# Holding the first expert's low-part subtracts back behind the first row gather, clearing two row tiles in mid-routing, and loading one pair of down weights later

## The chip, the cores and the metric

The kernel runs on one core of one Trainium2 chip. The metric is device time in microseconds (us) of one execution; 0.5% of it is 5.96 us. One execution was also taken by the hardware profiler, and its rows give start and length of each instruction on TensorE (PE, and PEld for its weight loads), VectorE (DVE), ScalarE (ACT), GpSimd (POOL) and SyncE (SP), and the landing of the transfers.

## The reference

A decoder block on x of 1024 rows by 1024 columns: a parallel pair of mixers (forgetting attention and a diagonal state space model), then a mixture of experts. Only the second half of it meets the change:

```python
def _hier_moe(x, w_rg, b_rg, w_re, b_re, w_gate, w_up, w_down):
    g_prob = jax.nn.softmax((xt @ w_rg) + b_rg)          # 4 groups
    g_top, g_sel = lax.top_k(g_prob, 1)
    e_prob = jax.nn.softmax(e_in)                        # 8 experts of that group
    e_top, e_idx = lax.top_k(e_prob, TOP_K)              # two of them
    w = g_top * e_top / jnp.sum(e_top, axis=-1, keepdims=True)
...
    for e in range(N_EXPERTS):                           # 32
        h = jax.nn.silu(xt @ w_gate[e]) * (xt @ w_up[e])
        y = y + combine[:, e:e + 1] * (h @ w_down[e])
# in the block:  x = x + mixed @ w_out;  x = x + _hier_moe(_rmsnorm(x, norm_ffn_g), ...)
```

An expert's gate and up weights are 1024x256 each, its down weights 256x1024.

## The kernel before

**Routing.** The output product `mixed @ w_out` runs over 8 row tiles of 128 rows, two halves of 512 columns each: 16 units, numbered `u`, one call of `product` each. Behind a tile's two units its `tail` runs: the finished rows go to `out_rows`, the norm's factor `rstd` is formed, the router's logits go through a long chain of small VectorE operations (group, two experts, position of the row within each expert), and the normed rows `xn` are stored to `xn_d` in DRAM. After the last tile the list `ix` is complete: for each of the 32 experts the numbers of up to 96 rows that chose it (line 1313).

**Experts.** They are taken in the order `ORDER`; "expert 0" below is the first in that order. For each: an indirect DMA on GpSimd's queue (`gather_rows`, L1330) fetches its rows of `xn_d` into a row tile `XG` that was cleared before (MEMSET, L1323); `turn_rows` transposes them on TensorE (L1341) and ScalarE and VectorE split the result into a high part `xh` (L1344) and a low part `xl` (L1345); `gate_up` multiplies them with the weights in three products: high x high (L1354), high x low weights (L1355), low x high (L1356), 24 matmuls in 8 steps; `hidden` forms `si` and `hh`; `down` multiplies with the down weights `wd` (L1379), and GpSimd adds the rows to `out_rows` (L1381, an indirect DMA too). Three row tiles rotate.

**Weights.** `load_expert` issues six loads of 512 KB on SP's queue for each expert: four `raw_e` (gate and up, L1085) and two `wd` (L1089). Five sets of buffers rotate. `split_expert` turns the four `raw_e` into high parts `weh` (8 casts on ScalarE, L1103) and low parts `wel` (8 subtracts on VectorE, L1104: raw less high). Once both have read a `raw_e` tile, the load of the expert five places later may overwrite it.

**Order.** The loads of the first experts start during routing, at the units that `AHEAD` lists ({unit: [(expert, loads)]}). `issue_after` (here through `after`) holds an instruction in its engine's stream until a named one has been issued; within an engine the order is then fixed. At routing's end, before: the two XG memsets, gather 0, gather 1, the third memset; on VectorE `ix`, `wts`, and then all of expert 0's subtracts.

Of the kernel before, what the change touches and what calls it, by code (L numbers as in the profile page):

```python
# [10 lines left out]
F32 = mybir.dt.float32  # L11
F32R = mybir.dt.float32r
# [4 lines left out]
ALU = mybir.AluOpType  # L17
AX = mybir.AxisListType

P = 128  # L20
D = 1024
S = 1024
# [20 lines left out]
def hybrid_block(ctx: ExitStack, tc: tile.TileContext, t, out):  # L43

    nc = tc.nc

    def pool(stack, name, bufs=1, side=None, space=None):
        kw = {}
        if side:
            kw["side"] = side  # L50
        if space is not None:
            kw["space"] = space
        return stack.enter_context(tc.tile_pool(name=name, bufs=bufs, **kw))
# [6 lines left out]
    def mmtile():  # L60
        return psA.tile([P, 512], F32, tag="A", name="psA_t")
# [4 lines left out]
    def f32(ap):  # L66
        return ap.bitcast(F32)
# [4 lines left out]
    def slot(name, shape=(S,), dt=F32, where=None):  # L72
        pl, n = where or (slab, SLOTS)
        return pl.tile([P] + list(shape), dt, tag="s4", name=name, bufs=n)
# [12 lines left out]
    sp = pool(ssm_stack, "ssm_c", 1, side="right")  # L87
# [265 lines left out]
    for nm, dst in (("ssm_C_re", Cre), ("ssm_C_im", Cim)):  # L353
        cin = tp.tile([P, 4, 2, 64], F32, name="cin", bufs=2)
        src = t[nm].rearrange("(b a) c p -> (a c) b p", a=8)
# [132 lines left out]
    with ExitStack() as st:  # L488
# [19 lines left out]
        for b in range(G // GB):  # L508
# [4 lines left out]
            v = wp2.tile([P, GB, P], F32, name="v", tag="t1")  # L513
# [79 lines left out]
            for q4 in range(GB // 4):  # L593
# [7 lines left out]
                for r in range(4):  # L601
                    g = q4 * 4 + r
                    o = ps[:, r * P:(r + 1) * P]
# [13 lines left out]
    with ExitStack() as st:  # L617
# [23 lines left out]
        for m in range(4):  # L641
            ms = slice(m * P, m * P + P)
            for n in range(2):
                ns = slice(n * 512, n * 512 + 512)
                ps = smtile()
                for k in range(4):
                    wh, wl = [w_[:, k % 2, ms] for w_ in wgl_[k // 2]]
# [332 lines left out]
    SR = (slabR, SLOTSR)  # L980
# [92 lines left out]
    def load_expert(e, raws, wd):  # L1073
# [13 lines left out]
        for j in range(2):  # L1087
            wd[j] = wd[j]()
            tc.keep_in_program_order(nc.sync.dma_start(wd[j], wd3[:, j, :]))  # L1089
            yield raws, wd  # L1090

    def split_expert(raws, c):

        ws = []
        for k2 in range(4):
            v = (2 * c + k2 // 2) % 3, k2 % 2
            if v not in ws_t:
                ws_t[v] = slot("weh", (2, 512), F32R), slot("wel", (2, 512), F32R)
            wh, wl = ws_t[v]
            for q in range(2):  # L1100
                src = raws[k2 // 2 * 2 + q][:, k2 % 2 * 2:k2 % 2 * 2 + 2, :]
                d_ = (slice(None), slice(None), slice(q * 256, q * 256 + 256))
                nc.scalar.copy(wh[d_], src)  # L1103
                nc.vector.tensor_tensor(wl[d_], src, f32(wh[d_]), ALU.subtract)  # L1104
            ws.append((wh, wl))
            if k2 == 1:
                yield
        yield ws
# [3 lines left out]
    def place_of(nm, shape, tiles, c, where):  # L1112
        def get():
            if c not in tiles:
# [7 lines left out]
    raw_t, wd_t, ws_t = {}, {}, {}  # L1122
    ahead = [load_expert(ORDER[o], [place_of("raw_e", (4, 256), raw_t, (SET[o], q), RAW[SET[o]][q]) for q in range(4)],
                         [place_of("wd", (S,), wd_t, (o % 5, j), WD[o % 5][j]) for j in range(2)]) for o in range(NE)]
    got = []
    AHEAD = {0: [(0, 6)], 2: [(1, 6)], 8: [(2, 6)], 12: [(3, 6), (4, 2)], 14: [(4, 2)]}

    ix = rp.tile([CAP, NE], I32, name="ix")
    wts = rp.tile([CAP, NE], F32, name="wts")
    empty = rp.tile([P, NE], F32, name="empty")  # L1130
    cnt = rp.tile([P, NE], F32, name="cnt")
    ptab = mmtile()
    with ExitStack() as st:
        xp = pool(st, "x1p", 1, side="right")
# [16 lines left out]
        def product(i, n):  # L1151
            if i not in x1s:
                x1s[i] = slot("x1", where=(SR, S2)[i - NT + 2]) if i >= NT - 2 else xp.tile([P, D], F32, name="x1", bufs=2)
                nc.gpsimd.dma_start(x1s[i], t["x"][i * P:(i + 1) * P, :])
            x1 = x1s[i]
            ns = slice(n * 512, n * 512 + 512)
            ps = mmtile()
            for k in range(KD):
                if k == KD // 2:
                    yield  # L1160
                mh, ml = [v[k // 4, i // 2][:, k % 4, i % 2 * P:i % 2 * P + P] for v in (mxh, mxl)]
                wh, wl = [v[:, k % 2, :] for v in wos[n, k // 2]]
                nc.tensor.matmul(ps, mh, wh, start=(k == 0), stop=False)  # L1163
                nc.tensor.matmul(ps, mh, wl, start=False, stop=False)
                nc.tensor.matmul(ps, ml, wh, start=False, stop=(k == KD - 1))
            nc.vector.tensor_tensor(x1[:, ns], ps, x1[:, ns], ALU.add)
# [113 lines left out]
        ends = {}  # L1280
# [3 lines left out]
        def behind_products(u):  # L1284

            if 0 < u <= len(units):
                i = units[u - 1][0]
                next(tails.setdefault(i, tail(i)))
            if u > 1 and units[u - 2] in done:
                next(tails[units[u - 2][0]], None)  # L1290

        done = [u for o, u in enumerate(units) if u[0] in [v[0] for v in units[:o]]]
        for u, (i, n) in enumerate(units):
            for o, m in AHEAD.get(u, ()):
                for _ in range(m):
                    r_ = next(ahead[o])
                got[o:] = [r_]
            pr = product(i, n)
            next(pr)
            if u == 1:  # L1300
                out_splits(3)
            behind_products(u)
            for _ in pr:
                pass
        behind_products(len(units))
        behind_products(len(units) + 1)
        for _ in range(2):
            r_ = next(ahead[4])

# [3 lines left out]
        last_dve = nc.vector.tensor_tensor(ix, ptab[0:CAP, 0:NE], empty[0:CAP], ALU.add)  # L1313
# [2 lines left out]


    em_ = pool(ctx, "moe", 1, side="right")
    XG = []

    def rows_tile(where):
        XG.append(where.tile([P, S], F32, name="XG") if where is em_ else slot("XG", where=where))
        nc.gpsimd.memset(XG[-1], 0.0)  # L1323

    rows_tile(SR)
    rows_tile(SR)
    mt = pool(ctx, "moet", 2, side="right")

    def gather_rows(xg, ix):
        return nc.gpsimd.indirect_dma_start(out=xg[0:CAP], out_offset=None, in_=xn_d[:, :],  # L1330
                                     in_offset=bass.IndirectOffsetOnAxis(ap=ix, axis=0),
                                     bounds_check=S - 1, oob_is_err=False)

    def turn_rows(xg):

        xh = mt.tile([P, KD, CAP], F32R, name="xh")
        xl = mt.tile([P, KD, CAP], F32R, name="xl")
        for kk in range(2):
            ps = smtile()
            for r in range(4):  # L1340
                pe = nc.tensor.transpose(ps[:, r * CAP:(r + 1) * CAP], xg[0:CAP, kk * 4 + r::8], ident[0:CAP, 0:CAP])  # L1341
            dst = (slice(None), slice(kk * 4, kk * 4 + 4))
            pv = ps[:, 0:4 * CAP].rearrange("p (a b) -> p a b", a=4)
            nc.scalar.copy(xh[dst], pv)  # L1344
            nc.vector.tensor_tensor(xl[dst], pv, f32(xh[dst]), ALU.subtract)  # L1345
        return (xh, xl), pe

    def gate_up(x, ws):
        xh, xl = x
# [40 lines left out]
    def icol(o):  # L1390
        return ix[:, ORDER[o]:ORDER[o] + 1]


    def after(*instructions):

        st = ExitStack()
        for ins in instructions:
            st.enter_context(tc.issue_after(ins.ins))
        return st

    for o in range(2):
        last_gather = gather_rows(XG[o], icol(o))
    with tc.issue_after(last_gather.ins):
        rows_tile(em_)
    w_now = got[0]
    got.append(r_)
    got.extend([None] * (NE - 5))

    def load(o, n):
        if o < NE:  # L1410
            for _ in range(n):
                got[o] = next(ahead[o])
    with after(ends["act"], last_dve):
        *_, ws = split_expert(got[0][0], 0)
    load(5, 4)
    x, _ = turn_rows(XG[0])
    sp = split_expert(got[1][0], 1)
    next(sp)
    load(6, 2)
    behind, act, dve = None, ends["act"], last_dve  # L1420
    scs = []
    for o in range(NE):
        if o + 2 < NE:
            gather_rows(XG[(o + 2) % 3], icol(o + 2))
        ps, pe = gate_up(x, ws)
        if o + 1 < NE:
            w_next = got[o + 1]
            if o:
                with after(act, dve):
                    sp = split_expert(w_next[0], o + 1)  # L1430
                    next(sp)
                load(o + 6, 2)
        h = hidden(ps)
        dve = next(h)
        if o + 1 < NE:
            with after(pe):
                x, pe = turn_rows(XG[(o + 1) % 3])
        if behind:
            with after(pe):
                _, sc, pe = down(*behind, apart=scs[-3:])  # L1440
            scs.append(sc)
            load(o + 4, 2)
        with after(pe):
            hT, act = next(h)
        e = ORDER[o]
        behind = (hT, w_now[1], icol(o), wts[:, e:e + 1])
        if o + 1 < NE:
            with after(act, dve):
                ws = next(sp)
            load(o + 6, 2)  # L1450
        w_now = w_next
# [13 lines left out]
    with tc.If(nb > 1):  # L1465
# [10 lines left out]
        with tc.For_i(1, nb, 1) as b:  # L1476
            with tc.For_i(0, NE, 1) as e:
                ne = nc.values_load(cnti[0:1, bass.ds(e, 1)], min_val=0, max_val=S)
                with tc.If(ne > b * CAP):
# [7 lines left out]
                    raws, wd = list(load_expert(e, [place_of("raw_e", (4, 256), raw_t, (0, q), None) for q in range(4)],  # L1487
                                                [place_of("wd", (S,), wd_t, (0, j), None) for j in range(2)]))[-1]
# [29 lines left out]
```

## Time and profile before

| what | value |
|---|---|
| median of 3 runs | 1191.19 us (1191.03 to 1195.45) |
| the profiled execution's own time | 1195.19 us |
| its span, first to last instruction | 1193.5 us (1.69 us lie around it) |
| PE busy | 1111.4 us, 93% of the span |
| DVE, ACT, POOL busy | 67%, 52%, 36% |
| bytes moved | 193.78 MB, mean 162 GB/s |

The profiled execution is 4.0 us (0.34%) longer than the median of the runs. The share of a busy engine is an average over very different stages: the routing ends at about 839 us, and the experts follow until the end.

### The profile page before, as it was taken

How to read it: one execution, taken by the hardware profiler on the slowest of the kernel's cores; microseconds unless marked ns; L12 is line 12 of the kernel's file. 1: busy time of each engine (PE TensorE's matmuls, PEld its weight loads, DVE VectorE, ACT ScalarE, POOL GpSimd, SP SyncE). 2: the span in 40 equal slices, each digit the busy share in tenths (PEclk: the TensorE clock that was granted, in tenths of full speed). 3: DMA queues.
4: the chain of work that ended last, by engine and by line, in shares of the span. 5: the costliest groups of instructions: out<-in, count | busy, mean ns of one | idle time of the engine just before them, and what ended most of it. 6: DMA issues, size and time to landing. Idle time of an engine off the chain costs nothing. (4 is left out here: it accounts for less than half of the span.)

```text
span 1193.5 us, 15934 instructions
## 1 busy us (share of the span) xinstructions
PE 1111.4 (93%) x5323; PEld 851.5 (71%) x5324; DVE 795.3 (67%) x1561; ACT 620.3 (52%) x1195; POOL 431.3 (36%) x431
## 2 busy tenths in 40 slices
PE   5999989899999999999899989998599999999995
PEld 4778877787898878888667767886366666666562
DVE  4976786575027889898986795538566666666661
ACT  5443232233226566756769453103466666666672
POOL 3143553541523564756624362103322222222211
PEclk9999999899999999999999998999699999999998
DMA  7625652330443020001523548564699999999992
GB/s 236 85 55 159 137 81 62 72 90 18 116 96 54 10 43 23 22 13 45 204 71 116 176 152 310 190 221 179 189 329 343 330 309 317 318 309 322 315 331 47
DMA packets 100918, 193.78 MB, mean 162 GB/s; under 512 B 26176, under 2 KB 55168, under 8 KB 100832
## 3 DMA queue, kind: packets, MB, share of 16 engines
q1 hardware_dynamic: 82176, 150.16, 41.1%
q0 software_dynamic: 14048, 34.17, 10.5%
q10 hardware_dynamic: 4608, 8.39, 1.9%
q8 instruction: 43, 0.70, 0.2%
q14 instruction: 43, 0.35, 0.1%
HBM read 164.30 MB, written 35.52 MB: 167 GB/s over the span
## 5 line engine op out<-in xcount | busy, mean ns | idle before, releaser
L1104 DVE TENSOR_TENSOR wel<-raw_e,weh 128x512 fp32r<-128x512 f32 x256 | 157.4, 687 | 118.1 <-ACT weh L1103 118.1
L1103 ACT CAST weh<-raw_e 128x512 fp32r<-128x512 f32 x256 | 137.1, 623 | 1.7 <-DMA raw_e<-in_w_expert_gate 1.3
L912 POOL TENSOR_TENSOR sm<-sm,pe 128x256 f32<-128x256 f32 (+2 forms) x80 | 96.3, 1204 | 69.5 <-ACT pe L909 61.3
L1379 PE MATMUL psA_t<-wd,hT 128*96 128x512 f32 x256 | 117.0, 600 | 2.7 <-DMA wd<-in_w_expert_down 1.9
L1354 PE MATMUL psA_t<-weh,xh 128*96 128x512 f32 x256 | 102.9, 402 | 0.2
L161 PE MATMUL psA_t<-hTh,wgl 128*128 128x512 f32 x256 | 101.8, 398 | 0.0
L160 PE MATMUL psA_t<-hTh,wgh 128*128 128x512 f32 x256 | 101.6, 397 | 0.0
L1355 PE MATMUL psA_t<-wel,xh 128*96 128x512 f32 x256 | 101.5, 396 | 0.0
L162 PE MATMUL psA_t<-hTl,wgh 128*128 128x512 f32 x256 | 101.3, 396 | 0.0
L1356 PE MATMUL psA_t<-weh,xl 128*96 128x512 f32 x256 | 100.6, 393 | 0.0
L1381 POOL DMA_INDIRECT out_rows<-R,ix x32 | 46.0, 1438 | 128.1 <-ACT hT L1370 116.9
L795 PE MATMUL psA_t<-wqh,hTh 128*128 128x384 f32 x256 | 87.9, 343 | 0.0
L796 PE MATMUL psA_t<-wql,hTh 128*128 128x384 f32 x256 | 86.3, 337 | 0.0
L797 PE MATMUL psA_t<-wqh,hTl 128*128 128x384 f32 x256 | 86.2, 337 | 0.0
L1330 POOL DMA_INDIRECT XG<-xn_d,ix x32 | 36.1, 1128 | 136.5 <-PE psB_t L1341 130.6
L1380 ACT ACTIVATE R<-psA_t,wts 96x512 f32<-96x512 f32 x64 | 43.8, 684 | 76.7 <-PE psA_t L1379 74.6
L1379 PEld LDWEIGHTS psA_t<-wd,hT 128*96 128x96 f32 x256 | 40.5, 168 | 55.6 <-issue 49.4
L907 ACT ACTIVATE pH<-psB_t 128x512 fp32r<-128x512 f32 (+1 forms) x96 | 49.2, 512 | 36.4 <-PE psB_t L904 36.2
L910 DVE TENSOR_TENSOR pL<-pe,pH 128x256 fp32r<-128x256 f32 (+2 forms) x80 | 63.0, 800 | 6.6 <-ACT pe L909 5.7
L160 PEld LDWEIGHTS psA_t<-hTh,wgh 128*128 128x128 f32 x256 | 48.5, 190 | 10.0 <-DVE uS L219 0.5
L161 PEld LDWEIGHTS psA_t<-hTh,wgl 128*128 128x128 f32 x256 | 48.7, 190 | 9.7 <-POOL wgl L150 0.2
L1163 PE MATMUL psA_t<-woh,mxh 128*128 128x512 f32 x128 | 54.3, 424 | 1.2 <-DVE gt L988 1.2
(427 smaller groups left out, 2867.8 us busy)
## 6 DMA issues: line engine op xcount, KB each, us to landing
raw_e<-in_w_expert_gate SPq DMA_DIRECT2D x64, 512.0 KB
raw_e<-in_w_expert_up SPq DMA_DIRECT2D x64, 512.0 KB
wd<-in_w_expert_down SPq DMA_DIRECT2D x64, 512.0 KB
gate_d<-ge ACTq DMA_DIRECT2D x32, 256.0 KB
gt<-gate_d SPq DMA_DIRECT2D x16, 512.0 KB
raw_g<-in_w_in SPq DMA_DIRECT2D x12, 512.0 KB
raw_q<-in_w_in SPq DMA_DIRECT2D x48, 128.0 KB
x<-in_x SPq DMA_DIRECT2D x8, 512.0 KB
```

Of the source, the lines that this page charges most:

```text
L160: nc.tensor.matmul(ps, wh, hTh[k][:, ns], start=(k == 0), stop=False)
L161: nc.tensor.matmul(ps, wl, hTh[k][:, ns], start=False, stop=False)
L162: nc.tensor.matmul(ps, wh, hTl[k][:, ns], start=False, stop=(k == KD - 1))
L795: nc.tensor.matmul(ps[:, :384], ah, wh, start=(k == 0), stop=False)
L796: nc.tensor.matmul(ps[:, :384], ah, wl, start=False, stop=False)
L912: nc.gpsimd.tensor_tensor(sm[:, o0:], sm[:, o0:], pe[:, :n], ALU.add)
L1103: nc.scalar.copy(wh[d_], src)
L1104: nc.vector.tensor_tensor(wl[d_], src, f32(wh[d_]), ALU.subtract)
L1354: nc.tensor.matmul(ps, xh[:, k, :], wh[:, k % 2, :], start=(k == 0), stop=False)
L1355: nc.tensor.matmul(ps, xh[:, k, :], wl[:, k % 2, :], start=False, stop=False)
L1356: last = nc.tensor.matmul(ps, xl[:, k, :], wh[:, k % 2, :], start=False, stop=(k == KD - 1))
L1379: pe = nc.tensor.matmul(po, hT[:, j, :], wd[j][:, ns], start=(j == 0), stop=(j == 1))
```

## The change

It has three parts. (1) Expert 0's weights are split by a new function, `split_first`, in three steps: its eight casts are issued where they were before, but the subtracts are held. A 128x1 memset of a new tile `tick` stands on GpSimd behind gather 0, VectorE copies `tick` onto itself and so waits for it; four of the subtracts follow, and the other four only behind the two `xl` of the first `turn_rows`. (2) Two of the three row tiles XG are placed and cleared at unit 8 of routing. (3) Expert 2's two `wd` loads leave unit 8 (`AHEAD[8]` asks for 4 loads of it instead of 6) and stand behind the last unit, ahead of expert 4's two `wd` loads.

```diff
+    def split_first(raws, c):
+        ws, low = [], []
+        for k2 in range(4):
...
+                nc.scalar.copy(wh[d_], src)
+                low.append((wl[d_], src, f32(wh[d_])))
+            ws.append((wh, wl))
+        for u in range(2):
+            yield ws
+            for l_ in low[4 * u:4 * u + 4]:
+                nc.vector.tensor_tensor(*l_, ALU.subtract)
+        yield ws
...
-    AHEAD = {0: [(0, 6)], 2: [(1, 6)], 8: [(2, 6)], 12: [(3, 6), (4, 2)], 14: [(4, 2)]}
+    AHEAD = {0: [(0, 6)], 2: [(1, 6)], 8: [(2, 4)], 12: [(3, 6), (4, 2)], 14: [(4, 2)]}
...
+            if u == 8:
+                rows_tile(SR)
+                rows_tile(SR)
...
         for _ in range(2):
+            next(ahead[2])
+        for _ in range(2):
             r_ = next(ahead[4])
...
-    rows_tile(SR)
-    rows_tile(SR)
...
-    for o in range(2):
-        last_gather = gather_rows(XG[o], icol(o))
+    tick = em_.tile([P, 1], F32, name="tick")
+    gather_rows(XG[0], icol(0))
+    nc.gpsimd.memset(tick, 0.0)
+    last_gather = gather_rows(XG[1], icol(1))
     with tc.issue_after(last_gather.ins):
         rows_tile(em_)
+    last_dve = nc.vector.tensor_copy(tick, tick)
...
-    with after(ends["act"], last_dve):
-        *_, ws = split_expert(got[0][0], 0)
+    with after(ends["act"]):
+        sp = split_first(got[0][0], 0)
+        ws = next(sp)
+    with after(last_dve):
+        next(sp)
+    x, _, dve = turn_rows(XG[0])
+    with after(dve):
+        next(sp)
     load(5, 4)
-    x, _ = turn_rows(XG[0])
```

GpSimd's stream at the end of routing (`x_...` and `xn_...` are row tiles, `rstd` the norm's factor), of the kernel before:

```order
L1271 DMA xn_d<-xn_8039 128x1024
L1202 DMA out_rows<-x_7565 128x1024
L1206 TENSOR_TENSOR rstd_7979<-rstd_7979,mhalf 128x1
L1276 TENSOR_TENSOR xn_8066<-xn_8066,gfB 128x512
L1323 MEMSET XG 128x1024 x2
L1330 DMA XG<-xn_d,ix 96x1024 x2
L1323 MEMSET XG 128x1024
```

The same place of the changed kernel:

```order
L1301 TENSOR_TENSOR xn_8066<-xn_8066,gfB 128x512
L1352 DMA XG<-xn_d,ix 96x1024
L1426 MEMSET tick 128x1
L1352 DMA XG<-xn_d,ix 96x1024
L1155 MEMSET XG 128x1024
```

The two memsets have left the place ahead of gather 0 (one now stands behind row tile 0's `rstd`, the other between the loads of two later row tiles), and the small one stands between the two gathers.

VectorE's stream from the row list on, of the kernel before:

```order
L1313 TENSOR_TENSOR ix<-psA_t,empty 96x32
L1314 COPY wts<-psA_t 96x32
L1104 TENSOR_TENSOR wel<-raw_e,weh 128x2x256 x9
L1345 TENSOR_TENSOR xl<-psB_t,xh 128x384
L1104 TENSOR_TENSOR wel<-raw_e,weh 128x2x256
L1345 TENSOR_TENSOR xl<-psB_t,xh 128x384
L1104 TENSOR_TENSOR wel<-raw_e,weh 128x2x256 x2
L1456 TENSOR_REDUCE nblk<-cnt 1x1
```

And of the changed kernel:

```order
L1344 COPY wts<-psA_t 96x32
L1487 TENSOR_REDUCE nblk<-cnt 1x1
L1492 CAST cnti<-cnt 1x32
L1489 TENSOR_SCALAR nblk<-nblk 1x1
L1490 TENSOR_SCALAR nblk<-nblk 1x1
L1493 CAST cnti<-nblk 1x1
L1430 COPY tick<-tick 128x1
L1108 TENSOR_TENSOR wel<-raw_e,weh 128x2x256 x4
L1367 TENSOR_TENSOR xl<-psB_t,xh 128x384 x2
L1108 TENSOR_TENSOR wel<-raw_e,weh 128x2x256 x4
L1123 TENSOR_TENSOR wel<-raw_e,weh 128x2x256 x4
```

Five tiny operations that before followed the twelve subtracts now stand ahead of the copy that waits; of the nine subtracts that stood directly behind `wts`, four stand behind that copy, four behind both `xl`, and the ninth, which is expert 1's, behind those.

SP's queue at the end of routing, of the kernel before (each `raw_e` load waits until its buffer has been read):

```order
L1278 DMA xn_d<-xn_8066 128x512
L1277 DMA xn_d<-xn_8066 128x512
L1089 DMA wd<-in_w_expert_down 128x1024 x2
L1085 DMA raw_e<-in_w_expert_gate 128x1024
```

And of the changed kernel:

```order
L1303 DMA xn_d<-xn_8066 128x512
L1089 DMA wd<-in_w_expert_down 128x1024
L1302 DMA xn_d<-xn_8066 128x512
L1089 DMA wd<-in_w_expert_down 128x1024 x3
L1494 TENSOR_LOAD cnti
L1494 ISA x2
L1085 DMA raw_e<-in_w_expert_gate 128x1024
```

Two more `wd` loads stand here, one of them ahead of the second store of the last normed rows, and a small read of a counter (`cnti`, which the tiny VectorE operations form) stands ahead of expert 5's loads instead of behind them.

## Rows read from the trace of the kernel before

**Rows 1.** The page: the span in 40 slices of 29.8 us, PE's busy tenths.

```profile
PE   5999989899999999999899989998599999999995
```

**Rows 2.** The waits of PE from 836 to 862 us: total, times, longest.

```profile
PE psB_t L1341 <- DMA XG<-xn_d,ix: 12.6, 1, 12.6
```

**Rows 3.** Timeline, 835 to 847 us: start, length, engine, line, tile, count [idle before].

```profile
835.56 5.28 ACT L1103 CAST weh<-raw_e 128x512 fp32r<-128x512 f32 x10
...
838.83 0.19 DVE L1313 TENSOR_TENSOR ix<-psA_t,empty 96x32 int32<-96x32 f32 x1 [0.60 <-PE psA_t L1265]
...
839.04 5.49 DVE L1104 TENSOR_TENSOR wel<-raw_e,weh 128x512 fp32r<-128x512 f32 x9
839.90 5.60 POOL L1330 DMA_INDIRECT XG<-xn_d,ix  x1 [5.33 <-DVE wel L1104]
840.95 0.33 SPq L1085 DMA_DIRECT2D raw_e<-in_w_expert_gate  x1
...
845.81 0.99 POOL L1330 DMA_INDIRECT XG<-xn_d,ix  x1 [0.30 <-DMA raw_e<-in_w_expert_up]
```

**Rows 4.** Tile XG: the gathers' lengths in ns, min/median/max.

```profile
L1330 POOL DMA_INDIRECT XG<-xn_d,ix x32: 952/975/5602, 839.9 to 1128.9; - x32
```

**Rows 5.** Transfers of three one-gather stretches (839, 848, 860 us): us from start to landing.

```profile
XG<-xn_d,ix POOLq DMA_INDIRECT x1, 11.3
...
XG<-xn_d,ix POOLq DMA_INDIRECT x1, 5.4
...
XG<-xn_d,ix POOLq DMA_INDIRECT x1, 4.1
```

**Rows 6.** Timeline, 832 to 835 us.

```profile
832.64 1.93 POOL L1323 MEMSET XG<- 128x1024 f32 x2
...
833.05 0.64 DVE L1264 TENSOR_SCALAR at<-iocap,pos 128x96 f32<-128x96 f32 x1
...
834.02 0.59 DVE L1225 TENSOR_SCALAR le<-gid,gf 128x32 f32<-128x32 f32 x1
```

**Rows 7.** Lines 1264 and 1225, all of each: lengths in ns, min/median/max.

```profile
L1264 DVE TENSOR_SCALAR at<-iocap,pos x16: 260/270/636, 745.7 to 837.9; 128x96 f32<-128x96 f32 x16
...
L1225 DVE TENSOR_SCALAR le<-gid,gf x8: 241/242/591, 740.8 to 834.0; 128x32 f32<-128x32 f32 x8
```

**Rows 8.** Timeline, 851 to 865 us: the first expert.

```profile
851.36 1.51 PE L1341 MATMUL psB_t<-ident,XG 96*128 96x96 f32 x8 [12.57 <-DMA XG<-xn_d,ix]
...
853.98 0.55 DVE L1345 TENSOR_TENSOR xl<-psB_t,xh 128x384 fp32r<-128x384 f32 x1
...
855.19 0.33 SPq L1085 DMA_DIRECT2D raw_e<-in_w_expert_gate  x1
...
856.86 0.40 PE L1355 MATMUL psA_t<-wel,xh 128*96 128x512 f32 x1
...
860.03 0.42 DVE L1364 TENSOR_TENSOR hh<-psA_t,si 96x256 f32<-96x256 f32 x1 [3.69 <-ACT si L1362]
...
864.07 0.33 SPq L1085 DMA_DIRECT2D raw_e<-in_w_expert_gate  x1
```

**Rows 9.** Windows: stretch and length; PE, PEld, DVE, ACT, POOL busy; PEclk, DMA share, GB/s.

```profile
834.50:840.30 5.80, 1.53 (x7) 0.92 (x6) 5.05 (x32) 4.85 (x11) 0.47 (x2) 0.50 0.72 226
...
850.50:855.50 5.00, 4.09 (x16) 2.97 (x17) 2.59 (x5) 3.09 (x5) 0.96 (x1) 0.57 0.34 82
...
861.50:864.50 3.00, 3.00 (x14) 2.10 (x13) 2.42 (x5) 3.00 (x7) 0.16 (x1) 1.00 0.34 93
864.50:923.00 58.50, 58.50 (x246) 36.53 (x245) 35.66 (x64) 40.36 (x82) 13.13 (x11) 1.00 1.00 334
```

**Rows 10.** Timeline, 922 to 925 us: an expert of the steady part.

```profile
922.56 3.10 DVE L1104 TENSOR_TENSOR wel<-raw_e,weh 128x512 fp32r<-128x512 f32 x5 [3.79 <-ACT weh L1103]
...
923.72 1.44 POOL L1381 DMA_INDIRECT out_rows<-R,ix  x1 [4.83 <-ACT weh L1103]
```

**Rows 11.** The waits of PE from 860 us to the end.

```profile
PE psA_t L1379 <- DMA wd<-in_w_expert_down: 1.9, 2, 1.4
```

More of the change, by code (lines that the diff above doesn't have):

```diff
@@ L1090, in load_expert @@
             yield raws, wd
+    def split_first(raws, c):
+        ws, low = [], []
+        for k2 in range(4):
+            v = (2 * c + k2 // 2) % 3, k2 % 2
+            ws_t[v] = slot("weh", (2, 512), F32R), slot("wel", (2, 512), F32R)
+            wh, wl = ws_t[v]
+            for q in range(2):
+                src = raws[k2 // 2 * 2 + q][:, k2 % 2 * 2:k2 % 2 * 2 + 2, :]
+                d_ = (slice(None), slice(None), slice(q * 256, q * 256 + 256))
+                nc.scalar.copy(wh[d_], src)
[6 more added lines that the diff above has]
+        yield ws
     def split_expert(raws, c):
@@ L1131, in hybrid_block, with rows_tile @@
     cnt = rp.tile([P, NE], F32, name="cnt")
+    XG = []
+    def rows_tile(where):
+        XG.append(slot("XG", where=where) if where is SR else where.tile([P, S], F32, name="XG"))
+        nc.gpsimd.memset(XG[-1], 0.0)
     ptab = mmtile()
@@ L1318, in hybrid_block @@
     em_ = pool(ctx, "moe", 1, side="right")
[L1319 to L1323, printed above, removed]
-    rows_tile(SR)
-    rows_tile(SR)
     mt = pool(ctx, "moet", 2, side="right")
@@ L1344, in turn_rows @@
             nc.scalar.copy(xh[dst], pv)
-            nc.vector.tensor_tensor(xl[dst], pv, f32(xh[dst]), ALU.subtract)
-        return (xh, xl), pe
+            dve = nc.vector.tensor_tensor(xl[dst], pv, f32(xh[dst]), ALU.subtract)
+        return (xh, xl), pe, dve
     def gate_up(x, ws):
@@ L1436, in hybrid_block @@
             with after(pe):
-                x, pe = turn_rows(XG[(o + 1) % 3])
+                x, pe, _ = turn_rows(XG[(o + 1) % 3])
         if behind:
```

## The prediction

> **What bounds the kernel now.** I read the slices of the page first. PE is nearly always at work [rows 1], except at the start, at the end and in the 29th slice (835 to 865 us), which shows 5 tenths: the passage from routing to the experts. The chain of work that ended last shows only the last scatter on this kernel, so I went on with the waits of PE in that passage. One wait stands out: 12.6 us, once, for the rows of expert 0 [rows 2]. Nothing else keeps PE there, and from 861 us on PE is busy without a gap until a wait of 1.9 us in all for down weights near the end [rows 11]. So what moves expert 0's rows moves the end, if that later wait does not take it back.
>
> The timeline tells why the rows are late [rows 3]. The list `ix` is done at 838.83 + 0.19 = 839.02 us. GpSimd's gather 0 starts at 839.90 and lasts 5.60 us; the median of the 32 gathers is 0.975 us and no other seems near 5.6 [rows 4]. Over just that time VectorE runs nine subtracts back to back, from 839.04 to 844.53 us. 844.53 + 0.975 = 845.505 us, and the gather ends at 839.90 + 5.60 = 845.50: it looks as if it did nothing until the ninth subtract was through and then took its normal time. ScalarE's casts start 3.5 us ahead of the subtracts, so VectorE never pauses between them. The rows land 11.3 us after the gather's start [rows 5], at 851.2 us, and PE starts its transposes at 851.36 [rows 8].
>
> **The change part by part.**
>
> *The two memsets leave the end of routing.* Two VectorE operations beside them are longer than elsewhere: L1264 takes 0.64 us and L1225 0.59 us [rows 6], where the medians are 0.27 and 0.24 [rows 7]; each ends with a memset. VectorE runs the chain to `ix` in order, so I take both, 0.37 + 0.35 = 0.72 us off. Bounds: 0 (if another engine's part of the chain comes last) and -0.72. In mid-routing the memsets cost two times 0.97 us of GpSimd, under products that keep PE busy; without that cover they would cost the same 0.72 there.
>
> *The subtracts are held.* Gather 0 then runs with no subtract beside it: 5.60 becomes 0.975, -4.63 us. VectorE does only the copy of `wts` and five tiny operations in that time. Gather 0 also started 0.88 us after `ix` was done, where gather 1 started 0.30 us after the one ahead of it [rows 3]; if that delay comes from the subtracts too, another 0.58 us goes. I take 0 for it, because nothing shows what it is.
>
> *The landing.* Behind the end of its instruction gather 0's rows took 11.3 - 5.6 = 5.7 us; the third gather's took 5.4 - 0.98 = 4.4 and the one at 860 us 4.1 - 0.95 = 3.15 [rows 4, 5]. In those 5.7 us expert 5's four `raw_e` loads, released by the subtracts from 840.95 us on, moved at the same time. In the changed kernel the subtracts, and so these loads, come behind the gather; instead the last of four `wd` loads are under way. I take the value in the middle, 4.4: -1.3 us; bounds 0 and -2.55.
>
> *Two more `wd` loads at routing's end.* From 864.5 us on the transfers fill all their time at 334 GB/s [rows 9], by which 512 KB take 1.57 us. One of the loads stands ahead of the store of half of the last normed rows, for which gather 0 waits. In the 5.8 us from 834.5 the transfers were busy 0.72 of the time, so 1.6 us were free and hold it: 0. If they don't: +1.6.
>
> *The subtracts in their new places.* One takes 5.49 / 9 = 0.61 us, four 2.44. The first four follow the copy of `tick` and are through before the rows land, 4.4 us after the gather. They can hold gather 1 back by 2.44 us; its rows are needed only when expert 0's 24 matmuls are through, so this is covered; without the cover it would be 2.44 us. The other four follow the second `xl`, which in the trace starts 2.62 us after PE's first transpose and ends at 3.17 [rows 8]. PE's first need of them is the 14th matmul, 856.86 - 851.36 = 5.5 us after that transpose, and it needs only two of them, done at 3.17 + 1.22 = 4.4; the last two are done at 5.6 and needed six matmuls later (58.5 us / 246 = 0.24 us each, 6.9). Even if all four had to be done for the 14th, PE would wait 0.1 us. Expert 1's four end at 8.05, ahead of `hh`, which stood at 860.03 - 851.36 = 8.67.
>
> *What the later subtracts release.* Expert 5's last two loads start at about 4.4 us after the first transpose, and expert 6's first two at 5.6 + 1.2 = 6.8, where before they started at 855.19 - 851.36 = 3.8. Four loads of 1.57 us from 4.4 on are through by about 10.9, and the next load is issued at 864.07 - 851.36 = 12.7. Before, the transfers were busy only 0.34 in the stretches 850.5 to 855.5 and 861.5 to 864.5 [rows 9], so there is room: 0. SP's read of the counter now stands ahead of expert 5's loads, but its operand is formed before the first subtract, so it is through when they are released: 0.
>
> *Sum.* -0.72 - 4.63 - 1.3 = -6.65 us. The profiled execution of 1195.19 us (span 1193.5 and 1.69 around it) would become 1188.5. It is 4.0 us above the median of the runs; against that median, 1191.19 - 6.65 = **1184.5 us**. With the bounds: at best -0.72 - 4.63 - 0.58 - 2.55 = -8.5, 1182.7; at worst 0 - 4.63 - 0 + 1.6 + 0.1 = -2.9, 1188.3.
>
> **The rivals.**
>
> *B: the gather is long by itself.* It is the first of its kind in the experts, and a burst of subtracts does not always hold GpSimd up: at 923.72 us a scatter started 1.16 us into such a burst and took 1.44 us [rows 10], all of it under subtracts. Then 5.60 us stay, wherever the subtracts stand, and only the memsets and the landing are gained: 1191.19 - 0.72 - 1.3 = 1189.2 us (1190.5 without the landing). Against it: the end falls on the ninth subtract's end plus one normal gather to 0.01 us, by chance once in some hundred times. The Trainium skill, "SBUF — State Buffer", section "Who interferes with whom", speaks for B: by it a `tensor_tensor` takes only the read interface of the pair shared with GpSimd, while forming DMA descriptors needs the write interface, so that `tensor_tensor` did not stall a DMA; the page calls the reason inferred. By that rule the sum would be B's 1189.2. The same section says that a VectorE operation with two inputs in SBUF does contend with a GpSimd instruction that reads SBUF, and the second to issue blocks until the first is through; a gather reads its list there, but by this it would wait for one subtract, not nine. The trace agrees with neither wholly.
>
> *C: the transfers take the gain back.* They are busy 1.00 from 864.5 us on [rows 9], and near the end PE waits 1.9 us for `wd` [rows 11]: weights arrive no earlier than the stream brings them. If its landings don't move, the last experts end when they did, at 1191.2 us. Against it: loads from 855 us on are released by subtracts and casts that follow expert 0's rows, and before 864.5 the stream has idle time; it decides only if that idle time is used up.
>
> *D, slower: the 1 MB moved to routing's end stands in the way.* Two loads that ran under routing now lie in the stream just ahead of gather 0's rows and of expert 5's weights. It decides if the stream has no idle time left between 834.5 and 864.5; then its end moves by 2 x 1.57 = 3.1 us, 1194.3 us, and if gather 0's rows must wait for all four `wd` loads, 6.3 us, 1197.5. Against it: 0.28 of the stretch from 834.5 and 0.66 of those from 850.5 and 861.5 are free.
>
> **How the numbers follow.** My forecast has 0.70, B 0.15, C 0.09, D 0.06. The time is that of the first, 1184.5 us, with its own range of 1182.7 to 1188.3. B has to be within for 8 in 10: 1182.6 to 1190.5, which leaves C and D out. About 0.5% (5.96 us) is what a measurement of this kernel can tell from no change, so faster means below 1185.2 and slower above 1197.1. The forecast lies 0.7 us under the first; of its range, weighed toward the sum, two thirds lie below: 0.46 faster. Of D the part with all four loads, 0.04, is slower. The rest, 0.50, is the same.
>
> **What would show it.** Gather 0 in the trace of the changed kernel: 0.97 us instead of 5.60, starting near 839.2 us. Its landing 4.4 us after its end; PE's one wait for the rows 12.6 - 5.9 = 6.7 us (its start moves with the memsets' 0.72). L1264's and L1225's new lines at 0.27 and 0.24 at the last row tile. No PE wait for the low weights in expert 0's 24 matmuls. A span shorter by 6.65 us and PE's wait for `wd` near the end still about 1.9 us. Wrong it would be if gather 0 stays above 5 us (B), if PE's waits for weights near the end grow by what was gained (C), or if the gather's rows land later than 851.2 us (D).

## The result, and the profile after

The changed kernel takes 1188.91 us (median of 10 runs, 1180.05 to 1190.69), the kernel before 1194.38 (10 runs, 1191.03 to 1197.9). The two medians differ by 5.5 us; the ratio on record for the two sets of runs is 0.9941, 95% interval 0.9921 to 0.9960: faster by 4.8 to 9.4 us, 7.0 in the middle, where 6.65 was forecast. The profiled execution took 1188.83 us with a span of 1187.1, against 1193.5.

The waits of PE in the passage [rows 2] and to the end [rows 11], after:

```profile
PE psB_t L1363 <- DMA XG<-xn_d,ix: 6.1, 1, 6.1
...
PE psA_t L1401 <- DMA wd<-in_w_expert_down: 3.6, 2, 2.3
```

The wait for expert 0's rows fell from 12.6 to 6.1 us; the wait for down weights near the end grew from 1.9 to 3.6. The timeline of the passage after, which answers to [rows 3] and [rows 6]:

```profile
830.68 0.26 DVE L1289 TENSOR_SCALAR at<-iocap,pos 128x96 f32<-128x96 f32 x1
...
831.65 0.23 DVE L1250 TENSOR_SCALAR le<-gid,gf 128x32 f32<-128x32 f32 x1
...
836.11 0.19 DVE L1343 TENSOR_TENSOR ix<-psA_t,empty 96x32 int32<-96x32 f32 x1 [0.60 <-PE psA_t L1290]
...
836.59 1.10 POOL L1352 DMA_INDIRECT XG<-xn_d,ix  x1 [6.43 <-DVE nblk L1487]
...
837.85 0.15 DVE L1430 COPY tick<-tick 128x1 f32<-128x1 f32 x1 [0.77 <-POOL tick L1426]
837.93 2.50 DVE L1108 TENSOR_TENSOR wel<-raw_e,weh 128x512 fp32r<-128x512 f32 x4
838.00 1.50 POOL L1352 DMA_INDIRECT XG<-xn_d,ix  x1 [0.18 <-issue]
...
842.14 1.51 PE L1363 MATMUL psB_t<-ident,XG 96*128 96x96 f32 x8 [6.07 <-DMA XG<-xn_d,ix]
```

Gather 0 lasts 1.10 us instead of 5.60. It starts 0.29 us after `ix` is done (836.30), not 0.88, and by the view of transfers its rows land 5.4 us after its start, 4.3 behind its end (5.7 before):

```profile
XG<-xn_d,ix POOLq DMA_INDIRECT x1, 5.4
```

From the start of `ix` to PE's first transposes 6.03 us pass, where 12.53 passed: 6.5 us. And one row does not fit the prediction's picture: gather 1 lies wholly under four back-to-back subtracts and takes only 1.50 us. The experiments go after it.

### The profile page after: what moved, and what is told of

Same layout as the page of the kernel before. It is cut to its first block, busy times and chain, and to the rows that moved or that the text cites. A ratio compares the mean times of both kernels' runs of the same rounds, so it can differ in the third digit from the quotient of the medians.

```text
span 1187.1 us, 15943 instructions
## 1 busy us (share of the span) xinstructions
PE 1110.9 (94%) x5323; PEld 849.5 (72%) x5324; DVE 796.3 (67%) x1562; ACT 620.1 (52%) x1195; POOL 426.7 (36%) x432
## 5 line engine op out<-in xcount | busy, mean ns | idle before, releaser
L1123 DVE TENSOR_TENSOR wel<-raw_e,weh 128x512 fp32r<-128x512 f32 x248 | 152.6, 687 | 119.9 <-ACT weh L1122 119.9
L1122 ACT CAST weh<-raw_e 128x512 fp32r<-128x512 f32 x248 | 132.9, 622 | 3.5 <-DMA raw_e<-in_w_expert_up 3.0
L1352 POOL DMA_INDIRECT XG<-xn_d,ix x32 | 31.9, 998 | 136.7 <-PE psB_t L1363 129.9
L857 DVE TENSOR_REDUCE mx<-psB_t 128x1 f32<-128x512 f32 (+2 forms) x96 | 51.2, 551 | 6.1 <-PE psB_t L855 2.7
```

## The experiments

The theory at this point: the hold is what shortens gather 0, and what PE gains there is partly given back at the end, where the weight stream is the bound. The rivals: the moved memsets did it; the gather was long by itself; the passage alone sets the gain.

**The changed kernel again** (no edit).

> The changed kernel once more. The theory on the passage: the gather of expert 0 lasts about 1.1 us and PE resumes about 6.0 us after the row list (12.5 before). The theory on the end: the weight stream is the bound from about 1100 us on, so the gain over the kernel before is less than the 6.5 us gained at the passage and varies from run to run, 3 to 8 us; its rival, that the passage alone sets the gain, expects 6 to 7 us in every round.

1188.11 us (12 runs), ratio 0.9938 (0.9914 to 0.9962): the gain stands. Its runs lie between 1181.54 and 1192.24 us. A stage table, from the timelines of this and other runs (us; `si` is ScalarE's first operation behind an expert's 24 matmuls):

| profiled kernel | `ix` | gather 0 | first transposes | `si`, expert 1 | last `si` | between the two | PE's waits for `wd` |
|---|---|---|---|---|---|---|---|
| before | 838.83 | 5.60 | 851.36 | 866.61 | 1171.86 | 305.25 | 1.9 |
| after | 836.11 | 1.10 | 842.14 | 858.71 | 1165.70 | 306.99 | 3.6 |
| again | 836.91 | 1.10 | 842.65 | 858.02 | 1166.05 | 308.03 | 5.7 |
| hold alone | 839.23 | 1.10 | 844.38 | 860.91 | 1172.08 | 311.17 | 6.5 |
| moves alone | 836.93 | 6.17 | 850.66 | 867.01 | 1172.44 | 305.43 | 2.0 |
| six loads fewer | 837.64 | 1.10 | 843.25 | 859.40 | 1160.56 | 301.16 | 0 |
| idle matmuls | 836.64 | 1.10 | 842.17 | 856.47 | 1165.63 | 309.16 | 3.9 |
| eight behind, idle matmuls | 836.67 | 1.10 | 841.88 | 856.28 | 1162.46 | 306.18 | 3.0 |

Each row is one execution. That of the hold alone, 1194.9 us, is the longest of its seven runs (the others took 1185.59 to 1189.07), so its last columns may not be typical.

**The hold alone**, and **the moves alone**. Edits against the changed kernel, the hold alone first:

```diff
-    AHEAD = {0: [(0, 6)], 2: [(1, 6)], 8: [(2, 4)], 12: [(3, 6), (4, 2)], 14: [(4, 2)]}
+    AHEAD = {0: [(0, 6)], 2: [(1, 6)], 8: [(2, 6)], 12: [(3, 6), (4, 2)], 14: [(4, 2)]}
-            if u == 8:
-                rows_tile(SR)
-                rows_tile(SR)
-        for _ in range(2):
-            next(ahead[2])
...
     em_ = pool(ctx, "moe", 1, side="right")
+    rows_tile(SR)
+    rows_tile(SR)
```

The moves alone:

```diff
-    gather_rows(XG[0], icol(0))
-    nc.gpsimd.memset(tick, 0.0)
-    last_gather = gather_rows(XG[1], icol(1))
+    for o in range(2):
+        last_gather = gather_rows(XG[o], icol(o))
...
-        sp = split_first(got[0][0], 0)
+    with after(ends["act"], last_dve):
+        *_, ws = split_expert(got[0][0], 0)
```

> Only the subtracts are held; the two memsets stand at routing's end and expert 2's down weights load at unit 8, as before. If the hold is what shortens the gather, it lasts 1.0 to 1.1 us here too and PE's wait for the rows is 6 to 6.5 us; L1264's and L1225's counterparts last about 0.6 us again. If the memsets matter for the gather, it stays above 2 us. Time: within 1 us of the changed kernel if the memsets and the moved loads are worth nothing.

> The memsets and expert 2's down weights stand where the change puts them, and the subtracts are not held: nine of them stand behind the row list again. The theory (the burst of subtracts holds the gather): 5.6 us for gather 0, PE's wait for the rows 12.5 us, and a time within 1 us of the kernel before. The rival (the gather was long for another reason that the earlier memsets took away): about 1.1 us.

The hold alone: 1187.93 us, ratio 0.9942 (0.9921 to 0.9963), gather 0 1.10 us. The moves alone: 1193.63 us, ratio 1.0001 (0.9983 to 1.0020), gather 0 6.17 us. So the whole measured gain is the hold's, and the moves change the time by no more than 2.4 us either way. The gathers, in the hold alone and in the moves alone:

```profile
840.30 1.10 POOL L1349 DMA_INDIRECT XG<-xn_d,ix  x1 [6.81 <-DVE cnti L1490]
```

```profile
837.14 5.49 DVE L1123 TENSOR_TENSOR wel<-raw_e,weh 128x512 fp32r<-128x512 f32 x9
...
837.44 6.17 POOL L1352 DMA_INDIRECT XG<-xn_d,ix  x1 [6.29 <-DVE wts L1344]
```

The memsets still show in the trace of the hold alone, in a place not foreseen:

```profile
830.40 1.30 POOL L1301 TENSOR_TENSOR xn<-xn,gfB 128x512 f32<-128x512 f32 x1 [0.83 <-ACT xn L1300]
830.50 3.02 DVE L1285 TENSOR_SCALAR te<-oh,ent 128x32 f32<-128x32 f32 x1
...
831.65 1.83 POOL L1155 MEMSET XG<- 128x1024 f32 x2
```

A VectorE operation of 0.23 us elsewhere stood for 3.02 us, until GpSimd's multiply and both memsets were through. From that multiply's start to `ix` it took 8.8 us here, 7.4 before and 7.1 with the moves alone (829.82 to 836.93).

**Four subtracts ahead of the waiting copy, and eight.** Against the changed kernel; with eight, a second `next(sp)` stands behind the first.

```diff
-    last_dve = nc.vector.tensor_copy(tick, tick)
...
     with after(last_dve):
         next(sp)
+        last_dve = nc.vector.tensor_copy(tick, tick)
```

> As the changed kernel, but four of expert 0's eight subtracts stand directly behind the row list, ahead of the copy that waits for gather 0. If gather 0 has to wait for the end of the whole burst, it lasts to 0.97 us behind the fourth subtract: about 2.5 us. If it only has to wait for the end of the subtract that runs when it starts, as gather 1 seems to in the changed kernel (1.50 us under four subtracts), it lasts at most 1.6 us. If the first gather is long by itself once subtracts run, however many, 5 us or more.

> As the kernel with four subtracts ahead of the waiting copy, but all eight of expert 0 stand there, behind one tiny VectorE operation (the reduce), so that gather 0 starts about 0.1 us after the first subtract, as with four. If gather 0 is held because the burst is long, it lasts to the end of the eighth subtract plus 0.97 us, about 5.7 us. If what counts is when it starts against the first subtract, it lasts 1.6 us, as with four.

With four the gather lasts 1.57 us, with eight 1.57 as well (1189.72 and 1194.78 us, one run each, too few to compare times). The rows with eight:

```profile
839.90 0.17 DVE L1486 TENSOR_REDUCE nblk<-cnt 1x1 f32<-1x32 f32 x1
840.01 4.90 DVE L1108 TENSOR_TENSOR wel<-raw_e,weh 128x512 fp32r<-128x512 f32 x8
840.11 1.57 POOL L1352 DMA_INDIRECT XG<-xn_d,ix  x1 [6.42 <-ACT weh L1102]
```

The first subtract has 0.5 us to go when the gather starts (840.01 + 0.61 - 840.11), and 1.57 is 0.5 more than the 1.10 of gather 0 without a subtract: the gather waited for that subtract and ran under the other seven. That a burst of subtracts holds a gather to its end is not so in general.

**Four, directly behind the copy of the weights.** Against the kernel with four, the tiny operations are sent behind the subtracts:

```diff
-                nc.vector.tensor_tensor(*l_, ALU.subtract)
+                ends.setdefault("low", nc.vector.tensor_tensor(*l_, ALU.subtract))
...
-    nc.vector.tensor_reduce(nblk[:, 0:1], cnt[0:1, :], axis=AX.X, op=ALU.max)
+    with after(ends["low"]):
+        nc.vector.tensor_reduce(nblk[:, 0:1], cnt[0:1, :], axis=AX.X, op=ALU.max)
+    with after(ends["low"]):
         nc.vector.tensor_copy(cnti[:, 0:NE], cnt[0:1, :])
```

> Four subtracts ahead of the waiting copy, directly behind the row list and the weights' copy, with no tiny operation between, so that gather 0 starts about 0.3 us after the first subtract, as in the kernel before (0.26 us after the second) and in the kernel with only the moves (0.31). If the start against the subtract counts, gather 0 lasts to the end of the fourth plus 0.97 us, about 3.1 us. If the length of the burst counts, 1.6 us as with the tiny operation between.

```profile
832.48 2.48 DVE L1108 TENSOR_TENSOR wel<-raw_e,weh 128x512 fp32r<-128x512 f32 x4
832.83 3.11 POOL L1352 DMA_INDIRECT XG<-xn_d,ix  x1 [6.33 <-DVE wts L1344]
```

3.11 us (1188.68 us in one run): 832.48 + 2.48 + 0.98 = 835.94 = 832.83 + 3.11. The gather is held to the end of the whole burst again, as in the kernel before. So both happen. What stands just ahead of the burst, or how late the gather comes, may decide. One more trait goes with it; the subtracts' lengths, with four held here, with eight (not held), and in the changed kernel at 844.7 us, where no held gather is near:

```profile
L1108 DVE TENSOR_TENSOR wel<-raw_e,weh x4: 678/678/680, 832.5 to 834.3; 128x512 fp32r<-128x512 f32 x4
```

```profile
L1108 DVE TENSOR_TENSOR wel<-raw_e,weh x8: 682/684/692, 840.0 to 844.2; 128x512 fp32r<-128x512 f32 x8
```

```profile
L1108 DVE TENSOR_TENSOR wel<-raw_e,weh x4: 681/686/689, 844.7 to 846.5; 128x512 fp32r<-128x512 f32 x4
```

Where the gather is held, the subtracts are a few ns shorter than in a burst that nobody disputes: 678 ns in the middle here and in the kernel before, 681 with the moves alone and with the earlier gather below, against 686.

**Eight subtracts behind the waiting copy**, **an earlier gather**, and **a later one**. The first moves the second `next(sp)` up behind the first; the second adds, to the moves alone, a gather at unit 8; the third, to the kernel with four directly behind the weights' copy, a tiny copy ahead of the burst and a memset that waits for it, and it drops the copy behind the burst.

The earlier gather:

```diff
             if u == 8:
+                nc.gpsimd.iota(ix[:, 0:1], pattern=[[0, 1]], base=0, channel_multiplier=1)
+                nc.gpsimd.indirect_dma_start(out=wts, out_offset=None, in_=t["w_router_expert"],
+                                             in_offset=bass.IndirectOffsetOnAxis(ap=ix[:, 0:1], axis=0),
+                                             bounds_check=S - 1, oob_is_err=False)
```

The later one:

```diff
+    with after(last_dve):
+        last_dve = nc.vector.tensor_copy(tick, cnt[:, 0:1])
-    gather_rows(XG[0], icol(0))
-    nc.gpsimd.memset(tick, 0.0)
+    ms = nc.gpsimd.memset(tick, 0.0)
+    with after(ms):
+        gather_rows(XG[0], icol(0))
```

> As the changed kernel, but all eight subtracts of expert 0 stand behind the copy that waits for gather 0, so that gather 1 meets a burst of eight instead of four. If a burst holds a gather until its end, gather 1 lasts about 5 us. If it is held for one subtract at most, about 1.5 us, as in the changed kernel. Gather 0: 1.1 us by either.

> As the kernel in which only the memsets and the down weights move (nine subtracts behind the row list), with one small gather of 96 router rows added in mid-routing, so that the gather of expert 0 is not the first of its kind in the program. If being the first makes it long, it lasts at most 1.6 us now. If the burst does, 5.6 us as before.

> Four subtracts ahead of nothing that waits, behind one tiny VectorE copy (as the reduce stood in the run with 1.57 us), and gather 0 held back by a tiny GpSimd memset that waits for that copy, so that it starts some 0.4 us after the first subtract. If what counts is how late the gather starts against the first subtract, it is held to the end of the fourth plus 0.97 us: about 3 us. If what counts is that a tiny VectorE operation stands between the copy of the weights and the burst, at most 1.6 us.

With eight behind the copy, gather 1 takes 1.50 us and gather 2, which starts 0.39 us after the fifth subtract, 1.14: not held (1187.91 us in one run). With an earlier gather in the program (1.09 us, at 672 us), gather 0 still takes 6.17 us (1198.46): it is not long for being the first, and with the 1.10 us of the runs that hold the subtracts, rival B of the prediction is out. The last run missed its aim: the program's order put expert 1's gather ahead of the memset, 0.19 us after the first subtract, and it took 1.48 us; expert 0's came second, and PE waited 10.7 us (1195.0 in one run). What it does show is one more gather let in, behind a tiny copy; the question that it was to settle stays open.

**Six loads fewer.** The down weights of the experts in places 10, 14 and 18 are not loaded.

```diff
-    def load_expert(e, raws, wd):
+    def load_expert(e, raws, wd, skip=False):
...
-            tc.keep_in_program_order(nc.sync.dma_start(wd[j], wd3[:, j, :]))
+            if not skip:
+                tc.keep_in_program_order(nc.sync.dma_start(wd[j], wd3[:, j, :]))
...
```

> The changed kernel without the down-weight loads of the experts in places 10, 14 and 18 (six loads of 512 KB; older weights stand in their place, so their part of the result is not computed). If the weight stream sets the end, PE's waits for down weights near the end (3.6 us in the profiled execution) vanish, and the time falls by 3 to 6 us against the changed kernel. If it doesn't, the time stays within 1 us.

1182.15 us, ratio 0.9860 (0.9831 to 0.9889): 6.0 us below the repeated run's median, some 9 us by the two ratios. PE has no wait for down weights, and from expert 1's `si` to the last one 301.16 us pass, 30 steps of 10.04. Every kernel with all loads takes longer there, and those that leave the passage sooner mostly take the longer: so near the end the stream is the bound. (The exception is the last row of the table, which leaves soonest and has 306.18; there expert 5's loads are released sooner too.)

The waits are not the whole of that loss. The kernel with the moves alone has one wait of 2.0 us and is 4.3 us behind the 301.16. Behind that wait it does six matmuls in 4.51 us, at a granted clock of 0.50 (1.2 GHz):

```profile
1121.99 4.51 PE L1401 MATMUL psA_t<-wd,hT 128*96 128x512 f32 x6 [1.98 <-DMA wd<-in_w_expert_down]
```

```profile
1124.00:1126.00 2.00, 2.00 (x4) 0.71 (x3) 0.00 (x0) 0.00 (x0) 0.00 (x0) 0.50 1.02 287
```

In the repeated run the same six take 2.82 us behind a wait of 2.00, and the clock stays at 1.00. So a wait of 2.0 us near the end cost another 1.7 in one execution and nothing in another.

**Idle matmuls**, and **eight behind with idle matmuls.** PE works in its wait; the second has all eight subtracts behind the waiting copy too, so that expert 5's loads are released sooner.

```diff
-                nc.tensor.matmul(ptab[0:CAP, 0:2 * NE], at, te.rearrange("p f e -> p (f e)"),
+                ends["pe"] = nc.tensor.matmul(ptab[0:CAP, 0:2 * NE], at, te.rearrange("p f e -> p (f e)"),
...
+    idle = mmtile()[0:CAP]
+    with after(ends["pe"]):
+        for k in range(12):
+            warm = nc.tensor.matmul(idle, ws[0][0][:, 0, 0:CAP], ws[0][0][:, k % 2, :], start=(k == 0), stop=(k == 11))
+    with after(warm):
+        x, _, dve = turn_rows(XG[0])
```

> The changed kernel with twelve matmuls that nobody reads, between the row list and expert 0's transposes, in PE's idle time. In the changed kernel the granted clock is 0.5 for the first 11 of expert 0's 24 matmuls, 0.43 us each instead of 0.24. If the idle time keeps the clock low, expert 0 has fewer or none of these, and PE is up to 2.2 us earlier from there on. At the end the stream theory expects under 1 us of that to be left, the other 1.5 to 2.2 us.

> The changed kernel with all eight subtracts behind the waiting copy and the twelve idle matmuls ahead of the transposes. PE should resume about 6 us after the row list at the full clock, and expert 5's and 6's loads start some 2 to 3 us earlier against PE than in the changed kernel. By the theory that the weight stream sets the end, an earlier and fuller stream gives 1 to 3 us against the changed kernel; if the end hangs on PE alone, up to 2.2 us, as for the idle matmuls alone.

The granted clock, in the changed kernel and with idle matmuls, from PE's first transposes on:

```profile
842.00:848.40 6.40, 6.21 (x19) 4.37 (x20) 4.72 (x9) 4.32 (x7) 0.96 (x1) 0.50 0.85 252
848.50:851.50 3.00, 3.00 (x14) 2.13 (x13) 1.08 (x2) 0.00 (x0) 0.00 (x0) 1.00 0.91 254
```

```profile
842.00:849.00 7.00, 6.58 (x31) 4.68 (x32) 5.51 (x10) 4.22 (x7) 1.29 (x2) 1.00 0.93 290
```

The changed kernel does expert 0's first 11 matmuls at the lower level (0.5, 1.2 GHz), 0.43 us apart; with PE at work in the wait the clock is at 2.4 GHz when the rows come, and from the first transposes to expert 1's `si` 14.3 us pass instead of 16.6 (15.4 in the repeated run). The time: 1186.6 us, ratio 0.9903 (0.9875 to 0.9932); with eight behind as well 1185.43, ratio 0.9912 (0.9884 to 0.9940). Both intervals overlap that of the changed kernel, so that they beat it is likely, by 1.5 to 2.7 us of median and 3 to 4 by the ratios, and not shown. With idle matmuls alone the end of the trace gave most of it back (309.16 between the `si`, 306.99 in the changed kernel); with eight behind as well it did not (306.18).

## Why the prediction was right, and where it was not

*The total*, -6.65 us, lies in the middle of the measured 4.8 to 9.4. It is not borne out term by term, and in part it fits by luck: up to PE's first transposes two terms miss by nearly the same, one way and the other (memsets and delay, below), and behind them two losses that the sum doesn't have (the lower clock and the end) stand against a gain that seems not to be the change's.

*The time*: 1184.5 us was forecast, from a median of three runs (1191.19); over ten runs the kernel before has 1194.38, and the changed one 1188.91. That is 0.6 us above the range that the forecast gives its own mechanism (1182.7 to 1188.3) and closer to rival B's 1189.2. It lies within the wider 1182.6 to 1190.5 only, whose upper end was put there for B, and B is out. Against the median of ten the sum gives 1187.7, 1.2 below what was measured. So the size of the change was forecast; that the time lies within the wider range is luck.

*The hold*: -4.63 predicted, -4.50 in the trace, and by the run with the hold alone it carries the whole gain. The reason given, that gather 0 did nothing until the ninth subtract was through, holds for this place in the program: 5.60, 6.17, 6.17 and 3.11 us, each ending 0.95 to 0.98 us after the burst. It does not hold for every burst: 1.57 us under eight. So the argument of rival B, that a scatter ran under subtracts [rows 10], was a true row with another meaning. The Trainium skill, "SBUF — State Buffer", section "Who interferes with whom", has the second to issue wait until the first is through: the runs with 1.57 and 1.50 us agree (one subtract's rest), the held ones don't (up to nine subtracts). What the Trainium skill says there of `tensor_tensor`, that it did not stall a DMA, does not carry over to this gather, 3.11 against 1.10 us; whether the forming of descriptors was held or the read of the list, no run here separates.

*The delay before the gather*, taken as 0 with 0.58 for a bound, was all gained (0.88 to 0.29). It does not come from the subtracts, as the prediction allowed: with the hold alone it is 0.88 again (839.42 to 840.30), with the moves alone 0.32 (837.12 to 837.44). So it goes with the moves; what it is stays open.

*The memsets*, -0.72: mis-sized. L1264's and L1225's counterparts fell to 0.26 and 0.23 as foreseen, but from GpSimd's multiply (831.39 before, 828.83 after) to `ix` it took 7.44 and 7.28 us: 0.16 gained. L1264's 0.64 had cost nothing: the large VectorE operation after it (L1274, L1299 after) starts 0.31 us behind L1264's start in both kernels. L1225's 0.35 came off, and some 0.2 was lost because another operation waited behind the multiply (L1234, 1.24 us instead of 0.26). The time of the run with the hold alone shows no loss without the moves. The rows before:

```profile
831.39 1.30 POOL L1276 TENSOR_TENSOR xn<-xn,gfB 128x512 f32<-128x512 f32 x1 [0.83 <-ACT xn L1275]
...
833.36 0.75 DVE L1274 SCALAR_TENSOR_TENSOR xn<-x,rstd,gfB 128x512 f32<-128x512 f32 x1
```

And after:

```profile
828.83 1.33 POOL L1301 TENSOR_TENSOR xn<-xn,gfB 128x512 f32<-128x512 f32 x1 [0.83 <-ACT xn L1300]
828.98 1.24 DVE L1234 SCALAR_TENSOR_TENSOR lg<-first,rstd,rbias 128x40 f32<-128x40 f32 x1
...
830.99 0.74 DVE L1299 SCALAR_TENSOR_TENSOR xn<-x,rstd,gfB 128x512 f32<-128x512 f32 x1
```

*The landing*, -1.3: 5.7 to 4.3, -1.4. The reason given fits the other runs. Behind gather 0's end the rows took 2.8 to 4.3 us in the seven executions in which the subtracts, and so expert 5's loads, come behind it, and 5.2 to 7.6 in the six in which subtracts stand ahead (before, moves alone, earlier gather, four, eight, four directly behind the weights' copy).

*Not in the sum*: expert 0 at the lower clock. Before, the clock was up after 4 of expert 0's 24 matmuls, after the change only after 11; the stretch from the first transposes to expert 0's `si` went from 8.3 (859.62 - 851.36) to 9.6 us (851.72 - 842.14). In the repeated run it was 8.4, so this cost comes and goes.

*The low weights*: right; PE has no wait for them.

*Rival C*, the transfers, at 0.09, was too cheap: it was treated as all or nothing, and it takes a part. The sign that the prediction names, a wait for `wd` still at 1.9 us, failed: 3.6, and 5.7 in the repeated run. The gain up to expert 1's `si`, counted from GpSimd's multiply, is 35.22 - 29.88 = 5.3 us in this pair; 306.99 - 305.25 = 1.7 of it went back at the end. That leaves 3.6, and the span gained 6.4; of the rest, 2.6 (831.39 - 828.83) lie before the first changed wait that the prediction speaks of. The moves alone show 1.6 us of the same (829.82) with a ratio of 1.0001, and executions of kernels that are the same up to there have that multiply anywhere from 825.19 (four, late) to 832.38 (eight). So I put the 2.6 down to the two profiled executions, not to the change; that is argued, not shown.

*Rival D*: the rows did not land later, as it has it, and the moves alone cost no time that the runs show. But the two `wd` loads at routing's end seem to delay the rows, a term that the prediction put at 0 with 1.6 for a bound: behind the gather's end the landing took 6.9 us with the moves alone against 5.7 before, and 3.5 to 4.3 in the kernels that hold the subtracts and move the loads against 2.8 with the hold alone. That is about 1 us, from one profiled execution of each.

## What to carry to other kernels

A gather that ends one normal length behind a burst of VectorE work was held by it here, though other gathers ran under such bursts: hold the burst back and look, rather than argue from the others. Before counting on a gain in the middle, look at what the end waits for: here a stream that was busy 0.98 of the time or more took 1 to 6 us back from every kernel with all loads that came early. Test the parts of a change apart; two of these three did nothing that the time shows.

## What the runs showed of the hardware

Two engines that contend may let each other in at the border of an instruction or not: a gather got in after one subtract of eight (1.57 us) and was held through four in another run (3.11 us), and a 0.23 us VectorE operation stood for 3.02 us behind three GpSimd instructions in a row, where before its like stood for 1.24 behind the first of them. The held gather goes with subtracts of 678 to 681 ns in the middle, the other with 684 to 686. Every held gather meets a burst directly behind the copy of `wts`; every gather let in behind the row list meets one directly behind a tiny operation. The start of the gather against the subtract then running is 0.07 to 0.19 us for those let in under a first subtract, and 0.26 to 0.35 for the held; but gather 2 at 0.39 us after the fifth of eight subtracts, let in, speaks against the start alone. These runs do not separate the two, and the cause stays open.
